# A two-layer hybrid trunk on one core: the same 10,923 instructions in an order found by 23 seeded re-schedulings

## Chip, cores and metric

One core of a Trainium2 chip. The number that counts is device time in microseconds (us) of one execution, as a median over runs; the profiled execution is one further run.

## What is computed

Two decoder layers over 1024 positions of width 1024. Each normalises its input, projects it once into eight column groups, runs three mixers on them and adds a projection of their gated outputs:

```python
h = _rms(x, norm_g)
q, k, v, ga, u, gs, xq, gx = split(h @ w_in)      # 512,128,128,512,512,512,512,512 columns
a = sliding_window_attn(rope(rms(q)), rope(rms(k)), v, sinks)   # 8 heads, 2 kv heads, window 128
s = s5(u, ...)            # 32 groups of 16 channels, complex diagonal scan, GELU, GLU
c = cross_attn(rms(xq), mem)                       # 4 heads of 128 into 256 memory tokens
x = x + concat(a * silu(ga), s * silu(gs), c * silu(gx)) @ w_out
```

All of it is float32. A large matrix product is three TensorE products, because each operand is split into a high part and a remainder (names with `h` and `l`: `hh`/`hl` the normalised input, `wh`/`wl`, `fh`/`fl`, `gh`/`gl`, `ph`/`pl` weights, `yh`/`yl` the SSM output): high by high, low by high, high by low.

## The kernel before

The model code does not issue instructions. Each call is recorded by a `Tape` with the instructions it depends on; `Tape.order()` then makes one list of all 10,923 of them (TensorE 6737, VectorE 1813, ScalarE 1099, GpSimd 581, DMAs issued by SyncE 693), and `Tape.issue()` emits them in that order, each engine's instructions pinned one behind the other. So every engine is one queue in program order, and the order of the list is all that decides what waits behind what.

`order()` is a list scheduler: it plays the program forward with the prices of `price()`, and at each moment every idle engine takes, among its instructions whose inputs are ready, the one with the lowest key. Keys are the order of recording, apart from a stage (`columns`, the gate and cross-query projections) whose other engines' work is brought forward by 10,000 and whose matmuls are put back by 2,500, so that they fill places where TensorE would otherwise wait. Those matmuls write PSUM tiles named `fc`; they are the filler of the whole kernel. `CAP` limits how many PSUM tiles of a kind are held at once. SBUF space is the table `PLAN`: a tag has a fixed list of slots used in turn, and a tile waits until the last user of the tile before it in its slot is done.

Every instruction in the trace therefore has the line in `issue()`, L333. Tiles are told apart by name. Those that matter here:

- `xt`, `nss`, `rsv`, `nr`, `nh`, `gb`: input rows, sum of squares, its scaled value, reciprocal root, normalised rows and gain of `norm_tile`; `nh` is transposed by TensorE into a `bg` bank and split into `hh`, `hl`. `set`, `wlt`, `wht` are scratch and table tiles filled by memsets on GpSimd (POOL).
- `tu`: a Toeplitz block of the SSM (`ssm_ops`), one for each of 8 eighths of the channels in a layer. TensorE's `tp` products give `kst` (VectorE), which goes out to `kscr` in DRAM, comes back shifted as `so`, and is copied by ScalarE into `tu`; TensorE then transposes or applies it (`bg<-tu`). `so` has one slot, so each load waits for the copy of the one before.
- `graw`, `gh`: output weights of group A by halves; `raw`, `wh`: the u columns of the input projection.
- `fg`, `gt`, `mg`, `xg`: gate values, written to DRAM and read back; `o0`, `o1`, `o2`: gated outputs of attention, SSM and cross-attention, split high and low (the last digit), the multiplication or subtraction on POOL. `o101` takes the SBUF slot of `hl11`, the low part of the second half of the normalised input, and so waits for the last `fc` product that reads it.

Of the kernel before, what the change touches and what calls it, by code (L numbers as in the profile page):

```python
# [3 lines left out]

# [14 lines left out]
P = 128  # L19
# [133 lines left out]
    return m << off, p0, p1  # L153


class Tape:


# [15 lines left out]
    def add(self, eng, name, fn, a, kw):  # L174
# [13 lines left out]
        for x, w in op.acc:  # L188
# [15 lines left out]
            seen.append((op.i, w, m, p0, p1))  # L204
            t["seen"] = seen
        op.cost, op.lat, op.mode = price(name, eng, out[0], ins, kw)
        self.ops.append(op)
        return op

    def order(self):  # L210

        ops = self.ops
        for op in ops:
            for x, _ in op.acc:
                if x.tensor.name in self.tiles:
                    op.pre.update(self.tiles[x.tensor.name]["before"])
            op.left, op.ready, op.tiles = len(op.pre), 0.0, []  # L220
            for j in op.pre:
                ops[j].post.append(op)
            for n in {x.tensor.name for x, _ in op.acc if x.space == bass.MemoryType.PSUM}:
                op.tiles.append(self.tiles[n])
        for t in self.tiles.values():
            t["left"], t["over"] = len(set(t["users"])), 0.0
            if t["slot"] in CAP:
                t["bank"] = None
        banks, held = {b: 0.0 for b in range(BANKS)}, dict.fromkeys(CAP, 0)
        owner = {}  # L230
        free = dict.fromkeys(self.ENGINES, 0.0)
# [6 lines left out]
        events, done, self.log, now = [0.0], [], [], 0.0  # L238
        freeing = []
        while len(done) < len(ops):  # L240
            assert events, "no instruction can go on"
            now = heapq.heappop(events)
            while events and events[0] <= now:
                heapq.heappop(events)
            while freeing and freeing[0][0] <= now:
                _, b, kind = heapq.heappop(freeing)
                banks[b] = now
                held[kind] -= 1
            for e in self.ENGINES:
                while waiting[e] and waiting[e][0][0] <= now:  # L250
                    r, k, i = heapq.heappop(waiting[e])
# [6 lines left out]
                back, op = [], None  # L258
                while ready[e]:
                    k, i = heapq.heappop(ready[e])  # L260
# [4 lines left out]
                    op = ops[i]  # L265
# [12 lines left out]
                t0 = now  # L278
                if e == "sync":
                    n = min(range(8), key=lanes.__getitem__)  # L280
                    free[e] = t0 + op.cost
                    pipe = max(t0 + 0.9, pipe) + op.mode
                    end = pipe + op.lat
                    lanes[n] = end
                else:
# [7 lines left out]
                    end = free[e] + op.lat  # L293
# [47 lines left out]
                last.setdefault(name, {})[op.eng] = ins  # L341


BANKS, CAP = 8, {"mm": 4, "kq": 2, "fc": 2, "tp": 2, "bg": 5}
HOP = 0.06
SWITCH = {(i, j): 0.1 if "half" in (i, j) else 0.0 for i in ("half", "one", "four") for j in ("half", "one", "four") if i != j}
# [2 lines left out]
def price(name, eng, out, ins, kw):  # L349

    n = 1
# [12 lines left out]
    if eng == "sync":  # L364
        size = 1
        for d in list(out.ap):
            size *= d[1]
        run = min((list(x.ap)[-1][1] if list(x.ap)[-1][0] == 1 else 1) for x in (out, ins[0])) * 4
        rate = 280e3 if run >= 2048 else 190e3 if run >= 512 else 110e3
        write = str(out.space).endswith("DRAM")  # L370
        return 0.45, 0.5 if write else 0.75, size * 4 / rate
    if eng == "scalar":
        c = 0.17 + 0.00083 * n if psum else 0.2 + 0.00083 * n
        if kw.get("accum_out") is not None:
# [2 lines left out]
    if eng == "vector":  # L377
# [6 lines left out]
        for x in ins:  # L384
            k = 1
# [3 lines left out]
        n = max(n, w)  # L389
# [1224 lines left out]
```

## Time and profile before

| what | value |
|---|---|
| median of 3 runs | 1267.82 us (1267.17 to 1268.06) |
| profiled execution, its own time | 1271.33 us |
| span of its instructions | 1269.6 us |
| mean granted TensorE clock | 0.995 |
| TensorE busy with matmuls | 1237.5 us (97%) |
| VectorE, ScalarE, POOL busy | 843.1, 544.9, 363.7 us |

The profiled execution is 3.5 us above the median; 1.7 us of it lie outside the span. Busy time of TensorE counts from the start of a matmul's record to its end, and records of matmuls that follow each other overlap, so that a busy share near 100% says that no gap was longer than that overlap.

### The profile page before, as it was taken

Reading aid. Unit: us, or ns where it says so; the run is one execution under the profiler, and the core shown is the slowest. Engines: PE = TensorE matmul, PEld = TensorE weight load, DVE = VectorE, ACT = ScalarE, POOL = GpSimd, SP = SyncE. Lnnn points to the kernel's source line nnn. Section 1 sums busy time; section 2 is a strip of 40 time slices with the busy share of each in tenths; the row PEclk is TensorE's granted clock in tenths of the full one; section 3 lists DMA queues with packets and bytes.
Section 4 is the critical chain, followed back from the end, with each engine's and each line's share of the span. In section 5 each row is a group of like instructions: output and inputs, shape, how many; then the busy total and the mean of one; then the engine's idle time right before and its main releaser. Section 6 shows DMA issues by size and latency. Waiting matters only on the chain.

```text
span 1269.6 us, 20347 instructions
## 1 busy us (share of the span) xinstructions
PE 1237.5 (97%) x7179; PEld 1046.1 (82%) x7179; DVE 843.1 (66%) x1941; ACT 544.9 (43%) x1320; POOL 363.7 (29%) x585
## 2 busy tenths in 40 slices
PE   8999999999999999899999999999999999899998
PEld 6987888898887988688878787899797897668886
DVE  6879889747788678632477888865787675444311
ACT  5463323336566666310344223344656575442100
POOL 1371010154342366310082100044342211283100
PEclk9999999999999999999999999999999999999999
DMA  8254545511225765773554555441313542377532
GB/s 245 62 138 114 150 138 170 145 45 54 85 77 153 212 184 150 214 224 125 183 136 114 145 145 147 120 113 42 105 35 124 174 131 76 98 235 244 177 108 75
DMA packets 190456, 171.79 MB, mean 135 GB/s; under 512 B 59625, under 2 KB 142097, under 8 KB 190354
## 3 DMA queue, kind: packets, MB, share of 16 engines
q1 hardware_dynamic: 190354, 170.48, 46.0%
q8 instruction: 57, 0.93, 0.3%
q14 instruction: 45, 0.37, 0.1%
HBM read 114.81 MB, written 46.72 MB: 127 GB/s over the span
## 4 chain that ended last, share of the span: by engine, by line
PE 82%; DMA 7%; DVE 4%; ACT 3%; POOL 2%; issue 2%; SPq 1%; DVEq 0%; ACTq 0%; POOLq 0%
PE mm L333 27%; PE fc L333 23%; PE bg L333 17%; PE kq L333 13%; DMA so<-kscr 3%; PE tp L333 2%; POOL o L333 1%; DMA raw<-in_w_in 1%; DMA x<-xr 1%; DMA xt<-x 1%; DMA graw<-in_w_out 1%; DMA gt<-gscr 1%; DMA gscr<-fg 1%; DVE hl L333 1%; SPq L333 1%
## 5 line engine op out<-in xcount | busy, mean ns | idle before, releaser
L333 PE MATMUL fc<-hh,fh 128*128 128x512 f32 x512 | 205.2, 401 | 2.0 <-DVE fg L333 1.6
L333 PE MATMUL fc<-hl,fh 128*128 128x512 f32 x512 | 205.7, 402 | 0.0
L333 PE MATMUL fc<-hh,fl 128*128 128x512 f32 x512 | 204.2, 399 | 0.1
L333 PE MATMUL mm<-ph,o 128*128 128x512 f32 x512 | 161.4, 395 | 0.0
L333 PEld LDWEIGHTS fc<-hh,fh 128*128 128x128 f32 x512 | 96.4, 188 | 21.7 <-DVE fg L333 2.4
L333 PEld LDWEIGHTS mm<-ph,o 128*128 128x128 f32 x512 | 95.9, 188 | 21.7
L333 PEld LDWEIGHTS fc<-hh,fl 128*128 128x128 f32 x512 | 96.7, 189 | 19.5 <-issue 1.2
L333 PEld LDWEIGHTS fc<-hl,fh 128*128 128x128 f32 x512 | 96.7, 189 | 17.1
L333 PE MATMUL kq<-ml,hh 128*128 128x256 f32 x384 | 109.2, 285 | 0.0
L333 PE MATMUL kq<-mh,hh 128*128 128x256 f32 x384 | 108.7, 286 | 0.0
L333 PE MATMUL kq<-mh,hl 128*128 128x256 f32 x384 | 108.7, 284 | 0.0
L333 PE MATMUL mm<-pl,o 128*128 128x512 f32 x256 | 101.1, 395 | 0.0
L333 PE MATMUL mm<-gh,o 128*128 128x512 f32 x256 | 85.4, 402 | 7.3 <-ACT gh L333 3.6
L333 POOL COPY ifs<-f 128x16 f32<-128x16 f32 x64 | 18.8, 315 | 209.8 <-PE tp L333 209.0
L333 DVE TENSOR_TENSOR xr<-xr,mm 128x512 f32<-128x512 f32 x32 | 21.9, 685 | 85.6 <-PE mm L333 85.5
L333 PEld LDWEIGHTS kq<-ml,hh 128*128 128x128 f32 x384 | 72.9, 190 | 1.4 <-issue 0.8
L333 PEld LDWEIGHTS kq<-mh,hh 128*128 128x128 f32 x384 | 72.7, 190 | 1.2 <-ACT aph L333 0.4
L333 PEld LDWEIGHTS kq<-mh,hl 128*128 128x128 f32 x384 | 72.7, 189 | 0.2
L333 ACT ACTIVATE apr<-apr,anm 128x256 f32<-128x256 f32 (+1 forms) x128 | 61.7, 484 | 19.9 <-DVE anm L333 19.8
L333 PEld LDWEIGHTS mm<-gh,o 128*128 128x128 f32 x256 | 48.7, 191 | 20.7 <-ACT gh L333 4.0
L333 PE MATMUL mm<-hl,wh 128*128 128x256 f32 (+1 forms) x192 | 62.8, 329 | 1.0 <-DVE hl L333 1.0
L333 PE MATMUL mm<-hh,wh 128*128 128x256 f32 (+1 forms) x192 | 60.8, 327 | 1.4 <-ACT wh L333 1.1
(259 smaller groups left out, 3001.0 us busy)
## 6 DMA issues: line engine op xcount, KB each, us to landing
fraw<-in_w_in SPq DMA_DIRECT2D x32, 512.0 KB
gscr<-fg SPq DMA_DIRECT2D x48, 256.0 KB
kraw<-in_w_mem_kv SPq DMA_DIRECT2D x16, 512.0 KB
xm<-mg SPq DMA_DIRECT2D x32, 256.0 KB
xr<-xm SPq DMA_DIRECT2D x32, 256.0 KB
praw<-in_w_out SPq DMA_DIRECT2D x16, 512.0 KB
mraw<-in_w_in SPq DMA_DIRECT2D x12, 512.0 KB
xt<-in_x SPq DMA_DIRECT2D x8, 512.0 KB
```

Source lines behind the costliest of these rows:

```text
L333: ins = op.fn(*map(self.real, op.a), **{k: self.real(x) for k, x in op.kw.items()}).ins
```

## The change

The scheduler body becomes `pass_(keys)`. `order()` runs it once for each of 23 seeds in `MOVES`, each time followed by `shift()`, and emits the order of a last pass. `shift()` looks at the pass's own log: it walks back from some of the TensorE instructions that started 0.12 us or more behind the one before, along the predecessors that were done last, and lowers their keys; and it adds a random offset to the keys of the tiles that some engine worked on in one stretch of time around such a place. Keys accumulate. Besides, `price()` charges more for some DMAs (a slower rate for a strided DRAM view on few partitions, 0.8 us more for strided sources and for copies from SBUF to SBUF). No instruction is added, removed or altered.

```diff
-            op.left, op.ready, op.tiles = len(op.pre), 0.0, []
+            op.tiles = []
...
+        keys = [op.key for op in ops]
+        for n in MOVES:
+            self.pass_(keys)
+            self.shift(keys, self.log, random.Random(n))
+        return self.pass_(keys)
+
+    def shift(self, keys, log, rnd):
+
+        ops, at = self.ops, {}
+        for t0, f, end, op in log:
+            at[op.i] = t0, f, end
+        step, share = rnd.choice((5.0, 20.0, 60.0)), rnd.choice((0.0, 0.0, 0.1, 0.4))
+        free, late = 0.0, []
+        for t0, f, end, op in log:
+            if op.eng != "tensor":
+                continue
+            gap, free = t0 - free, f
+            if gap >= 0.12:
+                late.append(t0)
+            if gap < 0.12 or rnd.random() >= share:
+                continue
+            o = op
+            while True:
+                keys[o.i] -= step * gap
+                if not o.pre or t0 - at[o.i][0] > 40.0:
+                    break
+
+                def over(j):
+                    return at[j][1 if ops[j].eng == o.eng != "sync" else 2]
+
+                o = ops[max(o.pre, key=over)]
+        if share and rnd.random() < 0.5:
+            return
+
+        w1, size = rnd.choice((5.0, 20.0, 60.0)), rnd.choice((5.0, 20.0, 80.0))
+        w0 = rnd.choice(late) - w1 * rnd.random()
+        some, engs = rnd.choice((0.1, 0.4, 1.0)), rnd.choice((self.ENGINES,) + tuple((e,) for e in self.ENGINES))
+        by = {}
+        for t0, f, end, op in log:
+            if op.eng in engs and w0 <= t0 < w0 + w1:
+                n = op.acc[0][0].tensor.name
+                if n not in by:
+                    by[n] = rnd.gauss(0.0, size) if rnd.random() < some else 0.0
+                keys[op.i] += by[n]
+
+    def pass_(self, keys):
...
+MOVES = (
+    100002, 100004, 100010, 100012, 100028, 100029, 100036, 100038, 100041, 100059, 100067, 100072,
...
-        write = str(out.space).endswith("DRAM")
-        return 0.45, 0.5 if write else 0.75, size * 4 / rate
+        dram = [x for x in (out, ins[0]) if str(x.space).endswith("DRAM")]
+        if any(len(x.ap) == 3 and x.ap[0][0] < x.ap[1][0] and x.ap[0][1] < P for x in dram):
+
+            rate = 150e3
+        lat = 0.5 if str(out.space).endswith("DRAM") else 0.75
+        src = list(ins[0].ap)
+        if len(src) == 3 and src[1][0] < src[2][1] or not dram:
+
+            lat += 0.8
+        return 0.45, lat, size * 4 / rate
```

In the listings of order that follow, the first number behind a tile's name is its number in the recording, which is the same in both kernels; the second is not. L333 is the kernel before, L389 the changed one.

The first place is GpSimd's queue at the start of the program, as it was:

```order
L333 IOTA set3_36_94 128x128
L333 MEMSET set3_177_114 128x1 x13
L333 MEMSET wlt_166_139 128x32 x2
L333 MEMSET wht_167_142 128x32 x2
L333 MEMSET set3_177_114 128x1 x10
L333 TENSOR_TENSOR nr_86_158<-rsv_87_154,mhalf_32_77 128x1
L333 MEMSET set3_177_114 128x1 x9
```

and as it is:

```order
L389 AFFINE_SELECT dsel_35_94<-dsel_35_94 128x16
L389 MEMSET set3_177_110 128x1 x32
L389 TENSOR_TENSOR nr_92_160<-rsv_93_158,mhalf_32_82 128x1
L389 MEMSET wlt_166_166 128x32 x2
L389 MEMSET wht_167_170 128x32 x2
L389 TENSOR_TENSOR nr_86_181<-rsv_87_176,mhalf_32_82 128x1
L389 MEMSET set0_17_122 16x448
```

All 32 memsets of `set3_177` now stand ahead of the first `nr`, and the memsets of `wlt` and `wht` behind it; `nr_92` (the tile of `xt1`) comes before `nr_86` (that of `xt0`).

The second place is TensorE's queue in the first layer's SSM, around the transposes of `tu_192` into `bg_216`, between `fc` products. Before:

```order
L333 MATMUL fc_308_1568<-hh01_81_196,fh_306_1416 128x512
L333 MATMUL fc_308_1568<-hl01_83_215,fh_306_1416 128x512
L333 MATMUL fc_308_1568<-hh01_81_196,fl_307_1429 128x512
L333 MATMUL fc_310_1622<-hh10_124_671,fh_306_1416 128x512
L333 MATMUL bg_216_1624<-tu_192_1064 128x128
L333 MATMUL fc_310_1622<-hl10_126_678,fh_306_1416 128x512
L333 MATMUL fc_310_1622<-hh10_124_671,fl_307_1429 128x512
L333 MATMUL bg_214_1530<-rx_206_1287,ef_182_1258 128x128
```

and now:

```order
L389 MATMUL fc_310_1622<-hh10_124_562,fl_307_1433 128x512
L389 MATMUL bg_214_1509<-rx_206_1291,ef_182_1166 128x128
L389 MATMUL bg_214_1509<-tu_184_1024 128x128
L389 MATMUL bg_214_1509<-rx_206_1291,ef_182_1166 128x128
L389 MATMUL bg_214_1509<-tu_184_1024 128x128
L389 MATMUL bg_214_1509<-rx_206_1291,ef_182_1166 128x128
L389 MATMUL bg_214_1509<-tu_184_1024 128x128
L389 MATMUL bg_214_1509<-rx_206_1291,ef_182_1166 128x128
L389 MATMUL bg_216_1641<-tu_192_1067 128x128
L389 MATMUL fc_310_1622<-hh10_124_562,fh_306_1419 128x512
```

The matmuls into `bg_214` that came behind `bg_216` now come ahead of it, and from the `tp_198` and `tp_199` products, from which the chain of `tu_188` starts, to `bg_216` there are 70 `fc` products where there were 56 (to `bg_215`, the one of `tu_188` itself, 54 where there were 42).

The third place is GpSimd's queue in the second layer's last third, where the gated outputs are made. Before:

```order
L333 TENSOR_TENSOR o001_2055_12047<-mg_2058_11031,o000_2054_12024 128x512
L333 TENSOR_TENSOR o011_2061_12090<-mg_2063_12057,o010_2060_12081 128x512
L333 TENSOR_TENSOR o101_1921_12111<-gt_1923_11501,o100_1920_12086 128x4x128
L333 TENSOR_TENSOR o201_1866_12123<-xg0_1893_11188,o200_1865_12094 128x4x128
L333 TENSOR_TENSOR o201_1866_12123<-xg1_1902_11766,o200_1865_12094 128x4x128
L333 TENSOR_TENSOR o001_2055_12047<-mg_2056_12088,o000_2054_12024 128x512
L333 TENSOR_TENSOR gt_1943_12125<-yh_1880_11405,yl_1882_11415 128x512
L333 TENSOR_TENSOR yl_1968_12178<-yt_1970_11669,yh_1966_12172 128x512
L333 TENSOR_TENSOR o101_1921_12111<-gt_1943_12125,o100_1920_12086 128x4x128
L333 TENSOR_TENSOR o201_1866_12123<-xg0_1932_12138,o200_1865_12094 128x4x128
L333 TENSOR_TENSOR o201_1866_12123<-xg1_1941_12151,o200_1865_12094 128x4x128
L333 TENSOR_TENSOR o001_2055_12047<-mg_2057_12167,o000_2054_12024 128x512
```

and now:

```order
L389 TENSOR_TENSOR gt_1923_11582<-yh_1880_11484,yl_1882_11494 128x512
L389 TENSOR_TENSOR xsc_1972_11797<-rsv_1973_11794,mhalf_32_82 128x4
L389 TENSOR_TENSOR o101_1921_11823<-gt_1923_11582,o100_1920_11787 128x4x128
L389 TENSOR_TENSOR o201_1866_11829<-xg0_1893_11264,o200_1865_11770 128x4x128
L389 TENSOR_TENSOR o201_1866_11829<-xg1_1902_11313,o200_1865_11770 128x4x128
L389 TENSOR_TENSOR gt_1943_11832<-yh_1880_11484,yl_1882_11494 128x512
L389 TENSOR_TENSOR xsc_1981_11882<-rsv_1982_11875,mhalf_32_82 128x4
L389 TENSOR_TENSOR yl_1968_11893<-yt_1970_11751,yh_1966_11878 128x512
L389 TENSOR_TENSOR o101_1921_11823<-gt_1943_11832,o100_1920_11787 128x4x128
L389 TENSOR_TENSOR yl_1968_11893<-yt_1989_11908,yh_1966_11878 128x512
L389 TENSOR_TENSOR gt_1953_11922<-yh_1881_11656,yl_1883_11668 128x512
L389 TENSOR_TENSOR o101_1921_11823<-gt_1953_11922,o100_1920_11787 128x4x128
```

The SSM outputs (`gt_1923`, `o101` from `gt_1923`, `gt_1943`, `gt_1953`) no longer have the attention outputs `o001` and `o011` between and ahead of them, which come later now; between `o101` from `gt_1923` and the end of `yl_1969` there were 27 other rows and there are 19. On TensorE the last `fc` product that reads `hl11` (tile `fc_1451`) stands in row 5364 of its listing, where it stood in row 5447, and ahead of the tiles `fc_1442` and `fc_1449`, which it followed.

## Rows read from the trace of the kernel before

**Rows 1.** The page: span, and busy time of each engine.

```profile
span 1269.6 us, 20347 instructions
...
PE 1237.5 (97%) x7179; PEld 1046.1 (82%) x7179; DVE 843.1 (66%) x1941; ACT 544.9 (43%) x1320; POOL 363.7 (29%) x585
```

**Rows 2.** Windows: stretch, length, busy time by engine, clock, DMA share, GB/s.

```profile
886.00:995.00 109.00, 109.00 (x744) 88.29 (x745) 82.95 (x305) 70.69 (x201) 32.49 (x42) 1.00 0.29 93
...
1050.00:1150.00 100.00, 92.03 (x425) 72.30 (x424) 46.87 (x85) 42.88 (x92) 45.05 (x37) 0.97 0.48 148
```

**Rows 3.** Waits of TensorE: total us, times, longest.

```profile
PE bg L333 <- ACT tu L333: 5.1, 8, 0.9
PE mm L333 <- ACT gh L333: 3.6, 1, 3.6
PE bg L333 <- DVE nh L333: 2.6, 3, 2.2
...
PE bg L333 <- ACT xpr L333: 1.8, 3, 0.8
...
PE mm L333 <- ACT wh L333: 1.1, 1, 1.1
PE mm L333 <- DVE hl L333: 1.0, 4, 0.4
```

**Rows 4.** TensorE timeline at 1105 us: start, length, what, idle before it.

```profile
1105.40 0.39 PE L333 MATMUL bg<-xph,xvh 128*128 128x512 f32 x1
1105.63 0.39 PE L333 MATMUL bg<-xpl,xvh 128*128 128x512 f32 x1
...
1108.81 0.50 PE L333 MATMUL mm<-gh,o 128*128 128x512 f32 x1 [1.88 <-DVE fg L333]
```

**Rows 5.** Windows at half clock and without waits (columns as in 2).

```profile
1110.30:1113.60 3.30, 3.30 (x10) 2.56 (x9) 1.91 (x3) 0.22 (x1) 2.42 (x2) 0.50 0.76 264
1160.00:1200.00 40.00, 40.00 (x175) 32.55 (x174) 17.36 (x22) 8.82 (x14) 11.39 (x9) 1.00 0.62 205
```

**Rows 6.** Timeline of the first 9 us (columns as in 4).

```profile
4.85 0.58 ACT L333 COPY gb<-bg 128x512 f32<-128x512 f32 x1 [1.84 <-PE bg L333]
5.33 1.06 ACT L333 ACTIVATE nh<-xt 128x1024 f32<-128x1024 f32 x1
...
6.51 0.15 DVE L333 TENSOR_SCALAR rsv<-nss 128x1 f32<-128x1 f32 x1 [2.99 <-ACT nh L333]
...
6.58 0.21 POOL L333 MEMSET wlt<- 128x32 f32 x2 [2.41 <-PE bg L333]
...
7.16 0.58 POOL L333 TENSOR_TENSOR nr<-rsv,mhalf 128x1 f32<-128x1 f32 x1
...
8.68 1.94 PE L333 MATMUL bg<-ident,nh 128*128 128x128 f32 x8 [2.16 <-DVE nh L333]
```

**Rows 7.** Timeline at the transposed u tiles, 126 to 132 us.

```profile
126.60 0.49 PE L333 MATMUL bg<-tu 128*128 128x128 f32 x2 [0.87 <-ACT tu L333]
126.65 0.56 SPq L333 DMA_DIRECT2D so<-kscr  x1
...
130.45 0.62 ACT L333 COPY tu<-so 128x512 f32<-128x512 f32 x1 [3.90 <-DMA so<-kscr]
...
131.12 0.49 PE L333 MATMUL bg<-tu 128*128 128x128 f32 x2 [0.84 <-ACT tu L333]
```

**Rows 8.** The chain that ended last: its piece at the gated output weights.

```profile
516.31 8.06 DMA graw<-in_w_out
```

**Rows 9.** POOL by window: stretch, its length, busy time, clock, DMA share, GB/s.

```profile
1060.00:1098.00 38.00, 2.02 (x2) 0.96 0.25 77
1103.00:1147.00 44.00, 36.29 (x30) 0.96 0.74 232
```

**Rows 10.** Timeline of POOL in the second layer's tail.

```profile
1098.02 1.27 POOL L333 TENSOR_TENSOR o<-mg,o 128x512 fp32r<-128x512 f32 x1 [14.15 <-PE fc L333]
...
1105.47 1.29 POOL L333 TENSOR_TENSOR o<-gt,o 128x512 fp32r<-128x512 f32 x1 [1.20 <-PE fc L333]
```

More of the change, by code (lines that the diff above doesn't have):

```diff
@@ L1 @@
 import heapq
+import random
 import math
@@ L153, in _spots @@
     return m << off, p0, p1
+class Stuck(Exception):
+    pass
 class Tape:
@@ L219, in order @@
                     op.pre.update(self.tiles[x.tensor.name]["before"])
-            op.left, op.ready, op.tiles = len(op.pre), 0.0, []
+            op.tiles = []
             for j in op.pre:
                 ops[j].post.append(op)
-            for n in {x.tensor.name for x, _ in op.acc if x.space == bass.MemoryType.PSUM}:
+            for n in sorted({x.tensor.name for x, _ in op.acc if x.space == bass.MemoryType.PSUM}):
                 op.tiles.append(self.tiles[n])
+        keys = [op.key for op in ops]
@@ L225, in order @@
+    def pass_(self, keys):
+        ops = self.ops
+        for op, k in zip(ops, keys):
+            op.key, op.left, op.ready = k, len(op.pre), 0.0
         for t in self.tiles.values():
-            t["left"], t["over"] = len(set(t["users"])), 0.0
+            t["left"], t["over"], t["real"] = len(set(t["users"])), 0.0, None
             if t["slot"] in CAP:
-                t["bank"] = None
+                t["bank"], t["prior"] = None, None
         banks, held = {b: 0.0 for b in range(BANKS)}, dict.fromkeys(CAP, 0)
@@ L240, in order @@
         while len(done) < len(ops):
-            assert events, "no instruction can go on"
+            if not events:
+                raise Stuck
             now = heapq.heappop(events)
@@ L341, in issue @@
                 last.setdefault(name, {})[op.eng] = ins
+MOVES = (
+    100002, 100004, 100010, 100012, 100028, 100029, 100036, 100038, 100041, 100059, 100067, 100072,
+    100088, 100099, 100280, 100299, 100385, 100390, 100397, 100423, 100427, 100432, 100443
+)
 BANKS, CAP = 8, {"mm": 4, "kq": 2, "fc": 2, "tp": 2, "bg": 5}
```

## Prediction

> **What bounds the kernel now.** First the page, for which engine is full. TensorE is busy 1237.5 of 1269.6 us and the next engine 66% [rows 1], so TensorE's queue is the time, and a new order can only win where that queue stands still. Visible idle is 1269.6 − 1237.5 = 32.1 us. The idle number understates a stop: matmuls of 512 columns start 0.23 us apart, but a record lasts 0.39 [rows 4], so about 0.39 − 0.23 = 0.16 us of every stop lies under the record before it. With some 36 stops that show, about 6 us are hidden that way.
>
> Next the windows by stage, for where the idle is. An attention stretch has 109.00 of 109.00 us busy, while 1050 to 1150 has 92.03 of 100 [rows 2]: a quarter of all idle in one place. Then the waits, which say what came last: the SSM's Toeplitz tiles 5.1 us in 8 stops, one stop of 3.6 at the gated weights, 2.6 for the norm, 1.1 and 1.0 for weights and normalised input [rows 3]. Last the clock. Three stretches of some 3.4 us, each behind idle spots, run at a granted clock of 0.50, the 1.2 GHz level: one of 3.3 us holds 10 matmul records, where at full clock 175 in 40 us make 3.3 × 175/40 = 14.4 [rows 5]. That is 4.4 × 0.23 = 1.0 us lost each.
>
> **The change, part by part.** Nothing is added or removed, so busy work is the same on every engine: no term there. Each term is a stop, and whether it goes is read from what the new queues put between the work that starts a chain and the matmul that waits for its end. I count matmuls between the two, times 0.23 us, against the time that the chain took in the trace.
>
> *Head.* The first norm tile is late: VectorE has `rsv` done at 6.51 + 0.15 = 6.66, but POOL starts `nr` at 7.16, behind memsets, and ScalarE starts the square at 5.33, behind a copy of `gb` from 4.85; TensorE stops for 2.16 us [rows 6]. Now the copy stands behind the square, the memsets of `wlt` and `wht` behind `nr`, and the first x tile is SyncE's first load. The POOL part alone is 7.16 − 6.66 = 0.50; with the ScalarE part up to 0.48 more, and the earlier load perhaps more, at most the stop of 2.16. I take 1.5. The moved memsets then lie on POOL beside TensorE's first products; if anything needs `wlt` sooner it costs their 0.2 us.
>
> *Normalised halves in the first layer.* Four stops for `hl`, 1.0 us [rows 3], with 4 × 0.16 hidden: 1.6. The transposes that feed them are now followed by 2.3 to 8 us of other matmuls, which is enough in three of the four: 1.4 (0 to 1.6).
>
> *Toeplitz tiles.* Eight stops, 5.1 us [rows 3], hidden 8 × 0.16 = 1.3: 6.4 at most. How one is made: the load of `so` is issued at 126.65, ScalarE copies it at 130.45, TensorE goes on at 131.12, 4.52 us after the previous tile's transposes at 126.60 [rows 7]. Between the two stood 14 `fc` products, 14 × 0.23 = 3.2 us; now 16 and the seven matmuls of `bg_214` stand there, 3.7 us and 7 short ones at about half that spacing, 4.5 together. That stop just about closes, as does the one ahead of it (54 products behind its root, not 42: 2.8 us more against a stop of 0.87). By the same count three more of the eight close, one closes by half, and two can't be told. I take 4, between 2 and 6.4. What is late next there is one further tile (`bg_251`) which has 18 products less between than it had; it goes among the new stops.
>
> *`wh` of the second layer.* One stop of 1.1 [rows 3] with 0.16 hidden; the matmuls between the load's release and the wait go from some 11.5 to 17.7 us. Gain 1.2 (0 to 1.3).
>
> *Gated weights.* The 3.6 us stop [rows 3] follows a load that took 8.06 us [rows 8] and could not be issued before its slot came free. SyncE's order there is unchanged, and the matmuls between are the same 7.2 us. Gain 0; if the weights came early after all, 3.6 + 0.16 and the half clock behind, 1.0: 4.8.
>
> *Tail, 1050 to 1150.* POOL is nearly empty first (2.02 of 38 us) and then full (36.29 of 44) [rows 9]: gated outputs can't start until slots come free, and its `o<-mg` stood idle 14.15 us and `o<-gt` 1.20 for an `fc` product of TensorE [rows 10]. That second product is the last that reads `hl11`, whose slot `o101` takes. Behind it one POOL multiplication after another is late and TensorE stops a dozen times, the longest 1.88 us [rows 4]. Now that product stands 83 rows earlier in TensorE's queue, 83 × 0.23 = 19 us, so `o101` can begin in the time in which POOL had nothing to do, and the SSM's chain has 19 rows in it, not 27; the eight that left are 1.3 us each [rows 10], 10 us less in the chain. The whole prize is idle 100 − 92.03 = 8.0 [rows 2], hidden 12 × 0.16 = 1.9, and two of the half-clock stretches, 2.0: 12. I take two thirds, 8, because `o001` and `o011` still have to be made by the same POOL, later: range 0 to 12.
>
> *New stops.* A rearranged queue makes new ones. Five chains that had enough work behind their root have less now, the transposed keys before the second layer's attention, the memory's key weights at the last quarter, one `xpr`, one softmax, and `bg_251`; each lost some us of cover and is now about as long as what it has. Nothing in the trace shows how late they will be; the nearest rows are the three `xpr` stops, 0.6 in the mean and 0.8 at most [rows 3], with 0.16 hidden 0.9. Five at 0.9 is 4.5, which I take off; 0 if the cover holds, 12 if as many others that I don't see come too.
>
> Smaller stops elsewhere: 0.7 gained. Sum: 1.5 + 1.4 + 4 + 1.2 + 0 + 8 + 0.7 − 4.5 = 12.3. The profiled run of 1271.33 would be 1259.0. It stood 3.5 above the median of 1267.82, so the median comes to 1255.5.
>
> **Rivals.** *All stops go.* 32.1 visible, 6 hidden and 3 × 1.0 of half clock are 41, all that there is, to 1227; the first loads and the last stores are in it and no order removes them, for which I leave 8 as an estimate: 33, giving 1235. For it: seven of eight groups of stops have more cover. Against it: the gated weights have none, and new stops. 5%. The Trainium skill, in "Trainium Kernel Development and Optimization", section "Performance Expectations", calls matmul busy time a bad metric and the weight-load share a good one; by that metric, with weight loads at 82% [rows 1], there would be room for some 220 us. The row of a stretch without any stop speaks against it: matmuls 40.00 of 40, weight loads only 32.55, which is 81% [rows 5]; so 82% is already what this kernel shows where nothing waits, and the rule's room isn't in reach of an order.
>
> *The stops move but stay.* Only the head is gained (1.5 and 1.4), and the tail and the Toeplitz tiles are bounded by POOL, ScalarE and the loads themselves, not by their place in the queue: what leaves one place arrives at the next. POOL full in 36.29 of 44 us [rows 9] speaks for it, its emptiness just before against it. 1267.82 − 2.9 + 2 of new stops = 1267, no change that a measurement of this kernel can tell (it agrees to about 0.2%, 2.5 us). 9%.
>
> *Slower, by the attention stretches.* There TensorE never stops (109.00 of 109) though VectorE is busy 82.95 and ScalarE 70.69 [rows 2]: cover in that stretch is what the old order got right. The new order spends some of it (the softmax chain among the five). Two layers of 2 × 8 units of attention, each with two pairs of heads, are 64 pieces that wait for a softmax in turn; if each comes 0.3 us late, that is 19 us against 16.8 of gains: 1270. It decides from 16.8/64 = 0.26 us a piece. Against it: of the chains there only a few have less cover, and a piece that is late gives `fc` work its place. 11%.
>
> *Half of the tail and Toeplitz gains*, 1262, is within the range of the likeliest, 75% together with it.
>
> **Numbers.** Forecast 1255.5, with its own bounds from the tail and Toeplitz terms (up to 8 + 2 slower, 4 + 2.4 faster) and the new stops (up to 7.5 slower, 4.5 faster). Not all fall to one side together; I take 8 either way, hence 1247 to 1263. To leave out no more than two in ten the range goes on to 1244 towards the case in which all stops go, and to 1266.5, the edge of no change. Faster by over 0.2% (below 1265.3): 0.8; within: 0.09; slower: 0.11.
>
> **What would show it.** Right: idle in the last 1050 to 1150 stretch (about 10 us earlier there) falls from 8 to under 3, the stretches at half clock fall from three to one; `bg<-tu` waits below 2 us in all; the first `bg<-ident,nh` starts 1 to 2 us sooner; the stop at `gh` still 3 to 4 us, with half clock behind it. POOL's `o<-gt` begins well before its `o<-mg` is through. Wrong: new stops of TensorE in the attention stretches (busy below 99% there), waits for `kx`, `xpr`, `kh` above 5 us together, or a POOL that is still full for 36 us at the end with TensorE stopping behind it, in which case the slots were not what held it.

## The result, and the profile after

The changed kernel takes 1256.26 us (median of 5, 1254.59 to 1258.18) against 1267.17 for the kernel before in the same session: a ratio of 0.9916 [0.9903, 0.9929], 10.9 us faster. The forecast was 1255.5. In the views PE is TensorE with its matmuls, PEld its weight loads, DVE VectorE, ACT ScalarE, POOL GpSimd and SPq SyncE's queue of DMAs; L with a number other than 333 or 389 is the line of `issue()` in an experiment's kernel. The page of the profiled run:

```profile
span 1254.5 us, 20325 instructions
...
PE 1231.1 (98%) x7179; PEld 1044.5 (83%) x7179; DVE 854.3 (68%) x1941; ACT 543.2 (43%) x1320; POOL 363.4 (29%) x585
```

Against [rows 1] the idle time of TensorE fell from 32.1 to 1254.5 − 1231.1 = 23.4 us, and its busy time by 6.4 us although the same 7179 matmul records stand there. The clock is not the main reason. Apart from the program's last few us, three stretches of 3.4 us ran at a granted clock of 0.50, the 1.2 GHz level, before, one of them shown in [rows 5] and the other two here:

```profile
526.55:529.95 3.40, 3.40 (x10) 2.66 (x9) 0.96 (x3) 0.30 (x1) 1.28 (x1) 0.50 0.74 241
1082.93:1086.33 3.40, 3.40 (x12) 2.93 (x11) 0.85 (x2) 0.30 (x1) 0.95 (x1) 0.50 0.21 77
```

In the stretch at 1110 us matmuls of 512 columns start 0.43 us apart, where at full clock they start 0.23 apart [rows 4]:

```profile
1111.01 0.63 PE L333 MATMUL kq<-yl,mh 128*128 128x512 f32 x1
1111.44 0.63 PE L333 MATMUL kq<-yh,ml 128*128 128x512 f32 x1
```

In the changed kernel it is as much time at half clock: 6.8 us from 86.2 us on, and 3.4 again at the gated weights:

```profile
526.49:529.89 3.40, 3.40 (x9) 2.65 (x8) 2.27 (x3) 0.03 (x1) 2.20 (x1) 0.50 0.84 283
```

So the two stretches in the tail are gone and two others came. Most of the 6.4 us is starts that come late by less than the overlap of two records: they count as busy, and only the table of lags below shows them. The waits of TensorE, which answer to [rows 3]:

```profile
PE tp L389 <- POOL ifs L389: 3.0, 3, 2.2
PE bg L389 <- DMA grow<-in_norm_g: 2.5, 1, 2.5
PE mm L389 <- ACT gh L389: 2.3, 1, 2.3
...
PE mm L389 <- ACT wh L389: 1.4, 1, 1.4
PE bg L389 <- ACT xpr L389: 1.2, 1, 1.2
...
PE bg L389 <- ACT tu L389: 0.4, 2, 0.2
...
PE mm L389 <- DVE hl L389: 0.2, 1, 0.2
```

Gone are the Toeplitz waits (5.1 to 0.4) and `hl` (1.0 to 0.2). The stop at the gated weights is still there, shorter (3.6 to 2.3), and so is that for `wh` (1.1 to 1.4). New at the top are three waits of `tp` for POOL's `ifs`. Windows, the first on the stretch behind those waits, then the two attention stretches and the tail, columns as in [rows 2]:

```profile
86.00:92.50 6.50, 5.78 (x19) 4.38 (x19) 3.94 (x6) 1.56 (x6) 6.50 (x16) 0.51 0.28 81
298.00:410.00 112.00, 111.91 (x764) 90.84 (x760) 87.52 (x312) 72.30 (x203) 36.09 (x51) 1.00 0.29 92
890.00:999.00 109.00, 109.00 (x761) 90.58 (x758) 83.67 (x307) 70.72 (x200) 32.69 (x42) 1.00 0.30 95
1044.00:1140.00 96.00, 92.36 (x454) 73.58 (x453) 69.56 (x107) 55.95 (x120) 57.84 (x49) 1.00 0.57 176
```

Attention shows next to no idle here either (the first layer's 111.91 of 112). The tail's idle is 96 − 92.36 = 3.6 us where it was 8.0. But 86 to 92.5 us runs at a granted clock of 0.51 behind the `ifs` waits.

At one and the same time two orders have done different work, so most of what follows goes by a table worked out from the traces, not by a view of the profile. Each matmul is given the usual spacing of its kind (the median from start to start between two of the kind, before's trace); the sum over the matmuls ahead is the *work* done, 1206 us in all, and the *lag* is a matmul's start less that sum. Lag grows only where TensorE stops, waits or runs slowly. Columns are the profiled runs of before, of the changed kernel and of experiments below:

```
work  before  after     e1     e2     e3     e4     e5     e9    e10    e12
  10    9.2    7.9    7.6    7.6    7.6    7.6    9.2    7.6    7.6    7.6
  75    6.8    3.2    5.3    2.8    5.3    2.8    6.9    5.2    5.3    5.3
 100    6.7    9.4    5.2    9.4    5.2    3.9    6.8    5.2    5.1    5.1
 240   10.0    9.8    7.3   10.1    7.7    4.3    9.9    8.0    7.3    7.6
 298   11.8   12.0    9.2   12.3    9.6    6.5   11.8    9.8    9.2    9.4
 410   18.0   20.6   15.3   21.4   15.5   15.2   18.0   15.8   15.3   15.5
 530   25.9   26.4   21.0   27.2   23.9   21.2   23.4   20.9   23.6   23.0
 700   29.5   28.7   23.9   30.6   28.0   24.4   25.9   23.8   26.5   27.3
 850   32.6   28.9   24.4   33.9   31.7   24.0   29.4   26.7   29.4   30.3
 990   42.1   35.3   30.6   43.3   40.5   30.3   38.9   36.2   38.9   39.8
1050   48.0   37.4   33.1   47.8   42.9   32.0   44.3   48.0   45.6   47.5
1100   57.0   41.6   38.4   56.4   48.0   36.3   51.8   59.3   52.9   51.6
1200   57.1   42.1   38.5   56.8   48.1   36.8   52.0   59.4   53.0   51.7
```

What counts as one kind is a choice. With kinds told apart by shape alone the differences between columns change by up to 0.4 us, except at work 75 (after and e2, by 2.5) and at work 1050 (e10, by 2.4), where the orders have done different kinds of work. A firmer comparison is a point at which two orders have done the same matmuls: the 496th starts at 75.27 us in the changed kernel, at 74.85 in e4 and at 77.41 in e3, which begins in the order of before.

By lag the profiled pair differs by 15.0 us, the medians by 10.9; the profiled run of before stood 3.5 us above its median. Runs e3, e9, e10 and e12 begin in the same order and have 1.6 us less at work 10 and 2 to 5 less at 530.

The head, which answers to [rows 6]:

```profile
4.57 1.06 ACT L389 ACTIVATE nh<-xt 128x1024 f32<-128x1024 f32 x1 [1.92 <-DMA xt<-in_x]
...
5.75 0.15 DVE L389 TENSOR_SCALAR rsv<-nss 128x1 f32<-128x1 f32 x1 [2.58 <-ACT nh L389]
...
5.99 0.58 POOL L389 TENSOR_TENSOR nr<-rsv,mhalf 128x1 f32<-128x1 f32 x1 [1.57 <-DVE rsv L389]
...
6.85 0.59 ACT L389 COPY gb<-bg 128x512 f32<-128x512 f32 x1 [1.13 <-PE bg L389]
...
7.54 0.75 DVE L389 SCALAR_TENSOR_TENSOR nh<-xt,nr,gb 128x512 f32<-128x512 f32 x1 [1.63 <-ACT gb L389]
...
8.45 1.11 PE L389 MATMUL bg<-ident,nh 128*128 128x128 f32 x4
```

`nr` starts 0.09 us after `rsv` (0.50 before), the square at 4.57 and not 5.33. But the gain vector `grow` is now loaded behind the first x tile, TensorE waits 2.5 us for it, the copy of `gb` ends at 7.44 (at 5.43 before), and the normalising product waits for that; so the first `bg<-ident,nh` comes at 8.45, only 0.23 us sooner.

The new stop:

```profile
82.82 0.60 POOL L389 COPY f<-cc 64x512 f32<-64x512 f32 x1
...
83.51 1.49 POOL L389 TENSOR_SCALAR f<-cc 64x512 f32<-64x512 f32 x1
...
85.07 0.60 POOL L389 COPY ifs<-f 128x16 f32<-128x16 f32 x2
...
85.32 0.92 PE L389 MATMUL tp<-ifs,es 128*128 128x144 f32 x4 [2.24 <-POOL ifs L389]
...
86.31 2.42 POOL L389 COPY ifs<-f 128x16 f32<-128x16 f32 x3
```

POOL makes `f` and the first `ifs` at 82.8 to 85.7, behind its whole chain of powers (`pm`, `pw`, `wlt`, `wht`). The kernel before had made them ahead of that chain:

```profile
49.37 0.60 POOL L333 COPY f<-cc 64x512 f32<-64x512 f32 x1 [2.50 <-DVE set L333]
...
52.91 0.67 POOL L333 COPY ifs<-f 128x16 f32<-128x16 f32 x4
57.00 0.70 POOL L333 TENSOR_TENSOR pm<-wlt,poles 128x64 f32<-128x64 f32 x2 [3.41 <-DVE poles L333]
```

They had to wait for `cn`, whose eight transposes stand here on TensorE:

```profile
66.56 1.04 PE L389 MATMUL bg<-ident,cn 128*128 128x128 f32 x8
```

In the kernel before they stand earlier:

```profile
43.18 1.04 PE L333 MATMUL bg<-ident,cn 128*128 128x128 f32 x8
```

The copies from them to `cc` and from there to `f` were late with them, and came behind the powers in POOL's queue.

POOL in the tail, which answers to [rows 10]:

```profile
1068.30 1.26 POOL L389 TENSOR_TENSOR o<-gt,o 128x512 fp32r<-128x512 f32 x1 [2.24 <-PE fc L389]
...
1073.48 1.32 POOL L389 TENSOR_TENSOR gt<-yh,yl 128x512 f32<-128x512 f32 x1 [1.38 <-DVE gt L389]
...
1077.72 1.29 POOL L389 TENSOR_TENSOR o<-gt,o 128x512 fp32r<-128x512 f32 x1
```

The first `o<-gt` (`o101`) starts at 1068.30 and not at 1105.47, and so do the three `o<-gt` behind it, 37 to 41 us earlier each.

### The profile page after: what moved, and what is told of

Same layout as the page of the kernel before. It is cut to its first block, busy times and chain, and to the rows that moved or that the text cites. A ratio compares the mean times of both kernels' runs of the same rounds, so it can differ in the third digit from the quotient of the medians.

```text
span 1254.5 us, 20325 instructions
## 1 busy us (share of the span) xinstructions
PE 1231.1 (98%) x7179; PEld 1044.5 (83%) x7179; DVE 854.3 (68%) x1941; ACT 543.2 (43%) x1320; POOL 363.4 (29%) x585
## 4 chain that ended last, share of the span: by engine, by line
PE 85%; DVE 4%; DMA 4%; POOL 3%; ACT 1%; issue 1%; SPq 0%; DVEq 0%; POOLq 0%; ACTq 0%
PE mm L389 27%; PE fc L389 25%; PE bg L389 17%; PE kq L389 13%; PE tp L389 2%; POOL pm L389 1%; DVE set L389 1%; DMA so<-kscr 1%; DMA graw<-in_w_out 1%; DVE hl L389 0%; DVE nh L389 0%; DMA raw<-in_w_in 0%; POOL o L389 0%; DMA gt<-gscr 0%; DVE gt L389 0%
## 5 line engine op out<-in xcount | busy, mean ns | idle before, releaser
L389 PE MATMUL fc<-hl,fh 128*128 128x512 f32 x512 | 205.8, 402 | 0.0
L389 PE MATMUL fc<-hh,fh 128*128 128x512 f32 x512 | 205.8, 402 | 0.0
L389 PE MATMUL fc<-hh,fl 128*128 128x512 f32 x512 | 205.2, 401 | 0.0
L389 PE MATMUL mm<-ph,o 128*128 128x512 f32 x512 | 161.4, 395 | 0.0
L389 PEld LDWEIGHTS mm<-ph,o 128*128 128x128 f32 x512 | 95.9, 188 | 22.4
L389 PEld LDWEIGHTS fc<-hl,fh 128*128 128x128 f32 x512 | 96.7, 189 | 19.5 <-issue 1.2
L389 PEld LDWEIGHTS fc<-hh,fl 128*128 128x128 f32 x512 | 96.7, 189 | 18.7
L389 PEld LDWEIGHTS fc<-hh,fh 128*128 128x128 f32 x512 | 96.8, 189 | 18.4
L389 PE MATMUL kq<-ml,hh 128*128 128x256 f32 x384 | 109.1, 285 | 0.0
L389 PE MATMUL kq<-mh,hh 128*128 128x256 f32 x384 | 108.5, 285 | 0.0
L389 PE MATMUL kq<-mh,hl 128*128 128x256 f32 x384 | 108.4, 283 | 0.0
L389 PE MATMUL mm<-pl,o 128*128 128x512 f32 x256 | 100.9, 395 | 0.0
L389 PE MATMUL mm<-gh,o 128*128 128x512 f32 x256 | 83.8, 403 | 3.2 <-ACT gh L389 2.3
L389 DVE TENSOR_TENSOR xr<-xr,mm 128x512 f32<-128x512 f32 x32 | 21.8, 685 | 92.7 <-PE mm L389 92.7
L389 POOL COPY ifs<-f 128x16 f32<-128x16 f32 x64 | 22.8, 375 | 207.6 <-PE tp L389 206.6
L389 PEld LDWEIGHTS kq<-ml,hh 128*128 128x128 f32 x384 | 72.3, 188 | 1.1 <-issue 0.8
L389 PEld LDWEIGHTS kq<-mh,hl 128*128 128x128 f32 x384 | 72.3, 188 | 1.1 <-issue 0.8
L389 PEld LDWEIGHTS kq<-mh,hh 128*128 128x128 f32 x384 | 72.1, 188 | 1.2 <-issue 0.8
L389 ACT ACTIVATE apr<-apr,anm 128x256 f32<-128x256 f32 (+1 forms) x128 | 61.7, 483 | 19.2 <-DVE anm L389 19.2
L389 PEld LDWEIGHTS mm<-gh,o 128*128 128x128 f32 x256 | 48.6, 191 | 16.1 <-ACT gh L389 2.7
L389 PE MATMUL mm<-hh,wh 128*128 128x256 f32 (+1 forms) x192 | 60.6, 329 | 1.4 <-ACT wh L389 1.4
L389 PE MATMUL mm<-hl,wh 128*128 128x256 f32 (+1 forms) x192 | 61.4, 328 | 0.2 <-DVE hl L389 0.2
```

What stands on the lines that cost most here:

```text
L389: ins = op.fn(*map(self.real, op.a), **{k: self.real(x) for k, x in op.kw.items()}).ins
```

## The experiments

All are run against the kernel before on the same chip, in four sessions (e1 to e4; e5 to e8; e9 to e11; e12) in which it had medians of 1266.91, 1267.37, 1267.16 and 1266.37. Gains in us are differences of medians; a ratio is estimated from all runs of a session, with its 95% interval, and can differ from that of the medians by some 0.1%. Where an experiment joins two orders, the kernel computes that of before (old DMA prices, one pass) and the changed one, takes the list of one up to a matmul, and behind it what is left in the order of the other; PSUM banks are given out again for the joined list by the rule of `pass_`.

**e1, e2, e3: where the gain is.**

```diff
-        return self.pass_(keys)
+        after = self.timed(keys)
+        # before: the list of the kernel before
+        return self.place(self.join((self.cut(before, 3400), after)))     # e1
+        return self.place(self.join((self.cut(after, 3400), before)))     # e2
+        return self.place(self.join((self.cut(before, 5448), after)))     # e3
```

> The order of the kernel before for everything that stands ahead of its 3401st matmul (just past the start of the second layer's projection, 618 us), and the changed order for the rest. Theory, gains are local: matched matmul for matmul, the changed kernel is level with the one before at that point (0.2 us behind) and gains 15 us after it in the two profiled runs, 11 by the medians. So nearly the whole gain: 1256 (1254 to 1258). Rival, the gain is made at the head and only kept: then the second layer alone gives what is left beside 3.7 us of head, 1260 or more. Rival, an order works only as a whole: 1264 or more.

> The changed order up to its 3401st matmul, the order of before for the rest. Theory, gains are local: level at the joint, so 1267 (1265 to 1269): 3.7 us gained in the first 75 us are given back by one new stop at 85 us and by the attention stretch. Rival, the head's gain is kept: 1263.5. The sum of the two halves' gains should be that of the whole.

> The order of before up to its 5448th matmul (991 us, late in the second layer's attention), the changed order behind. Theory, the tail's gain is local, from the earlier release of the slot that o101 takes and the shorter queue on POOL: the two profiles differ by 9 us from there on, so 1258 to 1260. Rival, POOL's work itself bounds the tail, and the changed kernel is faster there only because its SSM and its attention leave it other filler: 1265 or more.

Measured: e1 1253.21, ratio 0.9891 [0.9864, 0.9919]; e2 1271.05, 1.0036 [1.0019, 1.0054]; e3 1260.16, 0.994 [0.9921, 0.9958]. So the second layer's half of the new order gains more than the whole change (13.7 us), and the first layer's half loses 4.1; their sum, 9.6, is near the whole's 10.9. Both lie outside their expected ranges, by 0.8 and 2.1 us, e3 by 0.2. The rival that the head's gain carries the change is out. The last part alone, from the 5449th matmul on, gains 6.8 (by the ratio's interval 5.3 to 10). The rest of e1, some 7 us, is the second layer ahead of that: in the table its lag grows by 9.6 from work 530 to 990, that of before by 16.2.

**e4: what the stop at 85 us costs.**

```diff
+        after = self.ahead(after, [845, 846, 847, 848, 852, 853, 854, 855], 386)   # cn, TensorE
+        after = self.ahead(after, [849, 856], 498)                                 # cc, ScalarE
+        after = self.ahead(after, [857, 858, 951, 953, 959, 961], 860)             # f, ifs, POOL
```

> The changed order, but the eight transposes of cn go on TensorE at 43 us and not at 66, the two copies of them and POOL's two f and four ifs copies behind them ahead of POOL's chain of powers, where the kernel before has them. Theory, the new stop at 85 us (three waits for ifs, 3.0 us shown, 4.1 from start to start, and 1.6 of half clock behind them) comes from POOL getting to those copies last: all of it goes, 1250.6 (1249.5 to 1252.5). Rival, POOL's chain of powers, which the copies now lie in front of, becomes late instead and tp waits for es or the kst behind it: 1255 to 1257, no gain.

Measured: 1251.08, 0.9871 [0.9844, 0.9898], 5.2 us faster than the changed kernel was in its own session, and the fastest version of all. POOL makes `f` and `ifs` in an idle place, and TensorE no longer waits there:

```profile
51.01 0.60 POOL L474 COPY f<-cc 64x512 f32<-64x512 f32 x1 [2.64 <-issue]
51.70 1.50 POOL L474 TENSOR_SCALAR f<-cc 64x512 f32<-64x512 f32 x1
53.26 0.71 POOL L474 COPY ifs<-f 128x16 f32<-128x16 f32 x4
```

```profile
82.51 0.65 PE L474 MATMUL tp<-ifs,es 128*128 128x144 f32 x4
...
83.23 0.65 PE L474 MATMUL tp<-ifs,es 128*128 128x144 f32 x4
```

No `ifs` stands among the waits, which begin:

```profile
PE mm L474 <- ACT gh L474: 2.6, 1, 2.6
...
PE mm L474 <- ACT wh L474: 2.2, 1, 2.2
PE bg L474 <- ACT ef L474: 1.8, 2, 1.3
```

The cause of the new stop is shown. The rival, that the chain of powers becomes late instead, is out as to the time; of it there may be a rest in the waits for `ef`, 1.8 us where the changed kernel had 0.5.

**e5, e9, e10, e12: why the tail is faster.** The prediction had it that `o101` waits for the slot of `hl11`, and that releasing it earlier is the gain. e5 does that alone, for 57 of the 134 matmuls by which the changed kernel releases it earlier:

```diff
+        for k in range(27):
+            keys[7567 + k] -= 28.5      # fc_1444 and its gate value
+            keys[7624 + k] -= 84.5      # fc_1451; e9 and e10: 584.5
+        for k in range(10018, 10049):   # e10 only
+            keys[k] += 60
```

> The kernel before, with its own prices and one pass, but the keys of the gate columns fc_1444 and fc_1451 (the second half of the positions, with their gate values and stores) lowered so that both go ahead of fc_1442 and fc_1449; the first 9808 of its 10923 instructions are unchanged. fc_1451 then ends 57 rows earlier on TensorE, some 13 us, and the scheduler puts the o101 chain ahead of o001 on POOL by itself. Theory, the tail waits because hl11's slot is released last: a good part of the 9 us of the tail comes, 1259 to 1263, with POOL's first o from gt some 15 us earlier. Rival, the tail was gained by many small exchanges on all engines and this one does nothing alone: 1265 to 1269.

Measured: 1266.29, 0.9982 [0.9968, 0.9996]. `o101` did start 14 us earlier against the work (1088.3, in a run 3.2 us ahead) but 1.1 us is all that came by the medians (0.5 to 4.1 by the ratio's interval): the rival's range. A product of the gate chain, now early, waits for ScalarE's `gt`, which no wait of before's tail shows:

```profile
1091.07 0.50 PE L462 MATMUL kq<-yh,mh 128*128 128x512 f32 x1 [2.24 <-ACT gt L462]
```

> As the first-half-later version, but with the key of fc_1451 and its gate value lowered by 584.5 instead of 84.5: fc_1451 now ends at row 5956 of TensorE's queue, 132 rows earlier than in the kernel before and within two rows of its place in the changed kernel (5954); the first 9796 instructions are those of before. Theory, what pays in the tail is how early hl11's slot is released, and 57 rows were too few (they gave 1.1 us): most of the last part's 7 us, 1260 to 1262. Rival, the release is only one link, and the chain of the other half, o000 and o001 behind fc_1442 and fc_1449, and the last unit of cross-attention end late in its place: 1264.5 to 1267, with new waits at mm<-gh,o and kq<-yh.

> As the version with fc_1451 132 rows earlier, but also with the keys of the first chain of the last cross-attention unit (its norm, scores and softmax, tiles bg_2012 to bg_2019) raised by 60, so that its scores stand at row 6092 of TensorE's queue as in the changed kernel (6076) and not at 5984. Theory of the exchange, that work without a chain behind it must be left to cover the SSM's gate chain: 2 us or more faster than without it, 1260 to 1263. Rival, place of that unit doesn't matter: the same as without it, within 1 us.

Measured: e9 1274.2, 1.0064 [1.0043, 1.0086]; e10 1267.48, 1.0011 [0.9993, 1.0028]. The expectation of e9 was wrong about its own edit: `fc_1444` reads `hl11` too, and now stood behind `fc_1451`, at rows 5985 to 6008 of TensorE's queue, counted from 0, so the slot came free 80 rows earlier than before and not 132. POOL shows that it was still `fc` for which `o` waited:

```profile
1073.27 1.01 POOL L462 TENSOR_TENSOR xsc<-rsv,mhalf 128x4 f32<-128x4 f32 x1 [19.56 <-DVE rsv L462]
1087.55 1.26 POOL L462 TENSOR_TENSOR o<-gt,o 128x512 fp32r<-128x512 f32 x1 [13.27 <-PE fc L462]
```

In order of the release (row 6088 before, 6031 e5, 6008 e9, 5992 e10, 5954 in the changed kernel) the times are 1267.2, 1266.3, 1274.2, 1267.5 and, for e3, 1260.2. They do not follow the release. The place of one cross-attention unit is worth more: e10, whose keys differ from e9's in that unit alone (some 100 rows later), is 6.7 us faster. That is the 2 us or more which e10's theory asked for, but its time is not; and e9 is slower than theory and rival both allowed.

```diff
+        return self.place(self.join((self.cut(before, 5850), after)))     # e12
```

> As the version that takes the changed order for the last part, but joined later, behind the 5850th matmul (1054 us) instead of the 5448th: fc_1444 then stands whole right behind the joint (rows 5850 to 5874) and not spread over rows 5479 to 5596, and all from fc_1451 on is as in the changed kernel. Theory, the order of the last 400 matmuls before the tail's end, with both readers of hl11 and hl10 done and the second half of the gate products ahead of the last unit's softmax, is enough: 1259 to 1262, as with the early joint (1260.2). Rival, the gain was prepared earlier, by the 400 matmuls between the two joints, and a joint at 1054 us comes too late: 1264 or more.

Measured: 1265.29, 0.998 [0.9963, 0.9998]. The time is the rival's, although the slot of `hl11` is released at the changed kernel's own row (5954). Behind the joint TensorE waits for what the old order had not prepared:

```profile
1057.14 0.50 PE L464 MATMUL fc<-hh,fh 128*128 128x512 f32 x1 [1.17 <-DVE fg L464]
...
1063.90 0.50 PE L464 MATMUL fc<-hh,fh 128*128 128x512 f32 x1 [0.91 <-ACT fh L464]
...
1065.16 0.50 PE L464 MATMUL fc<-hh,fl 128*128 128x512 f32 x1 [0.53 <-DVE fl L464]
...
1071.46 0.50 PE L464 MATMUL kq<-yh,mh 128*128 128x512 f32 x1 [1.37 <-ACT gt L464]
```

Past that, from work 1050 to 1100, its lag grows by 4.1 us, as in the changed kernel (4.2) and e3 (5.1), where before has 9.0. From 990 to 1050 it grows by 7.7, before by 5.9, the changed kernel by 2.1, e3 by 2.4. So the tail's gain has two halves: some 4 us in the 400 matmuls from 991 us on, and some 5 us behind, where the gate chain is done before the `fc` products run out. In the first half the changed order spreads `fc` products among the waits of cross-attention (`fc_1444` over 130 rows, in e3 over 118, in before in one block of 36); that this spreading is what gains there is argued, no run changes it alone. The second half needs the first: without it (e12) 1.1 us is left of 6.8 by the medians, 0.3 to 4.7 by the ratio's interval. From the 5938th matmul on e12 and the changed kernel run level to within 0.5 us (the difference of matched starts is 9.7 us there, 10.1 at most and 9.7 near the end), so e12 loses nothing against it behind that point.

**e7, e8: what makes the order good.**

```diff
-MOVES = (
-    100002, ...
+MOVES = tuple(range(200000, 200023))      # e7
+MOVES = ()                                # e8
```

> The changed kernel with 23 other seeds (200000 to 200022), nothing else. Theory, what helps is which of these reshuffles were kept, not that keys of waited-for chains are lowered: 23 arbitrary ones leave the kernel no better than before, 1262 to 1285. Rival, lowering the keys of chains that TensorE waits for helps by itself, whatever the seeds: 1255 to 1260.

> The changed kernel with no seeds at all: one pass with the recording keys, as before, but with the new prices of the DMAs. Theory, the prices only shift when the scheduler believes a load has come and bring little alone: 1264 to 1269. Rival, the slower DMA price is what gives the Toeplitz loads their cover, and a third or more of the gain is here: 1263 or less.

Measured: e7 1272.92, 1.0044 [1.0026, 1.0061]; e8 1276.15, 1.0059 [1.0026, 1.0091]. The new prices alone make it slower by 0.6%, which neither side of e8's expectation had; 23 other seeds on top leave it there, as e7's theory said, and the kernel's own 23 bring it to 0.9916. One other set of seeds was run; how much sets differ is not shown. The waits of e8 begin with cross-attention and the SSM's gate inputs, at 480 to 500 us and from 1094 us on, in the tail:

```profile
PE bg L389 <- ACT xpr L389: 3.1, 2, 2.5
PE bg L389 <- DVE xpr L389: 2.7, 5, 0.9
PE kq L389 <- ACT yh L389: 2.6, 2, 2.0
```

**e6, e11: do the parts add?**

```diff
+        both = self.join((self.cut(after, 1648), self.cut(before, 3400), after))   # e6, after as in e4
+        return self.place(self.join((self.cut(after, 496), before)))               # e11, after as in e4
```

> The version with the early transposes of cn up to its 1649th matmul (297 us, the start of the first layer's attention), then the order of before up to its 3401st, then the changed order. Theory, gains are local and add: 2.7 us to be had ahead of the joint against the version whose first layer is that of before (1253.2), so 1250.5, and 2.5 less than the early transposes alone (1251.1) where the first layer's attention is worse in the changed order, less what the changed order gains at 410 to 505 us: 1249 to 1251. Rival, the joints cost as much as they bring, the filler being used up differently at each: 1252 or more.

> The order with the early transposes of cn up to its 497th matmul (75 us), that of before behind. The profiles put its gain at that point at 2.5 us against runs whose first 75 us are in the order of before, and 3.1 at 298 us. Theory, gains are local and kept: 1264 to 1265. Rival, what the head gains is lost at the next wait of the first layer, whose chain of powers on POOL and of tables on VectorE is no earlier: 1266.5 to 1268.

Measured: e6 1251.97, 0.987 [0.9845, 0.9894]; e11 1265.75, 0.9993 [0.9978, 1.0008]. e6 is no faster than e4 (1251.08): in its trace the first layer's attention is 2.5 us better (lag 12.7 at work 410 against 15.2), but it has only 0.8 of that left at work 700. The head alone can't be told from no change. Its lag is 3.0 at work 75, where runs in the order of before have 5.2 or 5.3, and 7.7 at work 240, where they have 7.3 to 8.0: by its time e11 lies between theory and rival, by its trace the rival holds: what the head gains is lost at the next waits, unless the order there changes too. e6 too lies between its two ranges.

## Why the prediction was right

The sign, the order of size and the main places of the gain were right. That the time came within 0.8 us (1255.5 against 1256.3) is luck: most terms of the sum were off, by up to 4 us, and cancel. Of the signs that the prediction named, idle in the tail fell to 3.6 and not under 3, `bg<-tu` to 0.4 as said, the first `bg<-ident,nh` came 0.2 us sooner and not 1 to 2, the stop at `gh` was 2.3 and not 3 to 4, and half clock did not fall from three stretches to one.

- *Head and `hl`*, 1.5 + 1.4 forecast: 2.0 to 2.5 at work 75, against runs that begin in the order of before. The step on the first norm tile failed: `nr` and the square are earlier, and the product then waits for `gb`; at the 244th matmul the changed kernel is level with e3 (41.37 and 41.38 us). The gain comes behind that, where the order of before waits for `hh` and `hl` and starts its first `fc` products late, and e11 shows none of it left at work 240 when the old order follows.
- *Toeplitz tiles*, 4 (2 to 6.4) forecast: 5.1 us of waits became 0.4. Lag from work 100 to 240 grows by 0.4 and not 3.3, from 700 to 850 by 0.2 and not 3.1: 5.8 in the profiled pair. Right in mechanism, undersized by 1.8 us. One size in it was misread: the seven matmuls of `bg_214` are not at half the spacing, they start 0.22 us apart in both traces, so they cover 1.6 us and not 0.8. The feared wait of `bg_251` did not come.
- *`wh`*, 1.2 forecast, 0 measured: wrong. TensorE reaches that place about as much sooner as the load does (issued at 645.69, before at 647.19), so products counted between release and wait did not show the wait. The load stands in SyncE's queue behind a row of small loads (`bn`, `cn`) that go out one behind the other, from 641.7 us before and 641.0 now, and these set its start.
- *Gated weights*, 0 forecast with 4.8 as the end: 1.3. The load took 7.00 us where [rows 8] have 8.06, at the same place in SyncE's queue. At least half of that is not the order's: in e1 and e3, which have the order of before up to there, the load took 7.35 and 7.30 and the stop was 2.87 and 2.83.
- *Tail*, 8 (0 to 12) forecast: 8.2 by lag from work 990 on, 6.8 by e3. Size right, reason only a part. The step that failed is "Now that product stands 83 rows earlier in TensorE's queue, 83 × 0.23 = 19 us, so `o101` can begin in the time in which POOL had nothing to do". The 83 are rows of a listing that merges like matmuls; the product stands 134 matmuls earlier, and starts at 1067.75 us and not at 1104.93. `o101` did begin 37 us earlier, but the release is not enough: e5 has 57 of the 134 rows and gains 1.1 us, e12 has all of them and gains 1.1. e3 and e12 show that the gain belongs to the whole stretch from 991 us. Which exchanges in its first 400 matmuls carry their half stays open, and so does whether the gain would come without the earlier release.
- *Half clock*, 1.0 us a stretch: undersized. At 0.43 us from start to start 8 matmuls of 512 columns fill 3.4 us, where the prediction counted the 10 records that touch the window, and 8 × (0.43 − 0.23) = 1.6 us are lost. By that estimate the two stretches that are gone from the tail are some 3 us of its gain.
- *New stops*, 4.5 forecast at five named chains: no wait for their tiles is longer than 1.2 us (an `xpr`). But lag grows by 2.4 us more in the first layer's attention, where TensorE is busy in 111.91 of 112 us: starts are late there by less than the overlap, and the sign that the prediction set (busy below 99%) can't see it. The real new stop, 6.2 us of lag and 5.2 by e4, stood where no cover had been counted, because only chains from TensorE to TensorE were, and this one is late on POOL's queue: and it could have been read from POOL's two listings, where the `f` and `ifs` copies move behind the whole chain of powers. With it came 6.8 us at half clock, two stretches' worth, where the prediction had one stretch left in all, at the gated weights.
- Unforeseen: the second layer's attention and its neighbourhood, where lag grows by 6.4 from work 850 to 990 and not 9.5. No run takes this stretch apart.

Of the rivals, the slower one named the attention of both layers; the first layer's did get slower, by 2.4 us, the second's faster. "Stops move but stay" holds for the first layer, whose half of the order is 4.1 us slower (e2). The rule of the Trainium skill weighed there ("Trainium Kernel Development and Optimization", section "Performance Expectations") would see the change in the weight-load share as 82% to 83%; idle and lag show where it came from, which the share does not.

## What to carry to other kernels

A new order is judged by matched work, not by the time in a trace and not by the busy share: take points at which both traces have done the same matmuls and watch where the lag grows. Here 6.4 of 15 us of lag lay in time that counts as busy. Read every engine's queue for an instruction that moved behind a long run of others, not only TensorE's; one such slip (six copies on POOL) cost half as much as the whole change gained, and putting it right by hand gave 1251.1 us. Here a buffer that was freed earlier was worth only what the rest of its chain let through: try such a release alone before it goes into a sum.

## What the runs showed of the hardware

Executions of one order differ in whether a stop is followed by 3.4 us at half clock. At the gated weights the profiled runs of before, e3, e10 and e12 fell to 0.50; those of e1, e5 and e9, with the same order up to there, did not. In e1 the clock stays at 1.00 through the stop and behind it:

```profile
522.00:527.00 5.00, 4.78 (x21) 3.91 (x22) 3.84 (x5) 1.22 (x2) 1.30 (x1) 1.00 0.92 321
```

Lag at work 530 is 20.9 to 25.9 in runs of that one order. That is more than most single terms here, so one profiled pair does not size them. And POOL's `ifs` copy, 128x16, took 0.20 us in the median in the traces of before and after, but 0.68, 1.20 and 0.66 at 86.3 to 88.7 us in the changed kernel, while VectorE worked on tiles of 512 and 1024 columns (`ef<-ef,es`, `fl<-fraw,fh`, `es<-wht,wlt`); single copies of 0.65 us and more occur elsewhere in both kernels.
